# Half-steps in three 256-column matmuls a block, one block of output columns after the other

## The chip, the cores and the metric

The kernel runs on one core of one Trainium2 chip. The metric is the device time of one execution, in microseconds (us); shorter is better. A core has a matrix engine (PE; its weight loads are listed apart as PEld), a vector engine (DVE), a scalar engine (ACT), a general engine (POOL) and a queue that issues transfers (SP). They run side by side and wait for each other through semaphores. PE writes its sums into PSUM, eight banks of 512 float32 columns on each of 128 partitions; everything else lies in SBUF.

## What is computed

A decoder trunk of two layers over 256 tokens of width 1024. Each layer is a half-step, a mixer (latent attention in layer 0, forgetting attention in layer 1), a second half-step and a gated embedding. The part that the change is about, cut from the reference:

```python
def swiglu(x, w_in, w_out):                 # D_MODEL 1024, D_FF 2816
    gate, up = jnp.split(x @ w_in, 2, axis=-1)
    return (jax.nn.silu(gate) * up) @ w_out

for i in range(DEPTH):                      # DEPTH 2
    h = h + 0.5 * swiglu(rms_norm(h, g_ffn1[i]), ffn1_w_in[i], ffn1_w_out[i])
    h = h + mixer(rms_norm(h, g_mix[i]))    # latent (i = 0) or forgetting (i = 1)
    h = h + 0.5 * swiglu(rms_norm(h, g_ffn2[i]), ffn2_w_in[i], ffn2_w_out[i])
    h = h + sigmoid(rms_norm(h, g_ple[i]) @ ple_w_gate[i]) * (p[i] @ ple_w_proj[i])
```

All inputs are float32. There are four half-steps, and in each the products with `w_in` and `w_out`.

## The kernel before

**Three products for one.** Each float32 factor is split into a high part (rounded to fp32r) and a low part (the rest): a weight into `whi` and `wlo`, an activation into two planes `x[:, k, 0]` and `x[:, k, 1]`, 256 tokens each, next to each other in SBUF. A product is hi·hi + hi·lo + lo·hi, and low times low is dropped. The residual `h` is kept transposed, features on partitions and the 256 tokens in the columns, so a weight block of 128 rows by 128 output columns is the stationary operand (loaded by LDWEIGHTS), and the activation streams past it. What follows calls one weight block, at one k (row of blocks) and one b (block of output columns), simply a block.

**Weights.** `Weights` cuts all weights into units, mostly 1024 rows by 256 columns (8 k by 2 b, 16 blocks). `_load` brings a unit in on SP's queue, `_split` makes `whi` by ACT (L86) and `wlo` by DVE (L87) in pieces of 1024 columns. There are six buffers of each, three units' worth. `get()` hands out the next unit and first lets the unit two further on be split, so a split waits for the buffers of the unit just used.

**A half-step** is `ffn` (L423). Stage one runs over f = 0..10: a unit of gate columns and a unit of up columns, 8 k each, summed in PSUM. `part` (L420) calls `by_width` (L238): first all high blocks, k outside and the two b inside, each in one matmul of 512 columns that streams both activation planes into a bank of its own (hi·hi in the left half, hi·lo in the right, L255); then all low blocks in matmuls of 256 columns onto the right half (L248). `wide` (L417) gives a PSUM tile of two banks for that, one for the gate and one for the up unit; the pool `psa` has two such tiles. `summed` takes a result out: ACT copies the left halves (L431), DVE adds the right halves, and DVE and ACT go on from SBUF (`gate`, `product`). The products are split again into `hid`. Stage two runs over dp = 0..3, 256 output columns each, 22 k in units of 8, 8 and 6, in the same way from `hid`; its result is summed, scaled, added to `h`, and `after.chunk(dp)` prepares two rows of the next norm's input `xa`.

The kernel opens with f = 0 of the first half-step, in chunks of two k as `x` is turned (L1120 and after); its eviction follows once the root mean squares are known.

**Elsewhere** the kernel already uses `mm_w` (L231), three matmuls of 256 columns a block: hi·hi and hi·lo with the high block, loaded for each, and lo·hi. This is so in the latents `zmm` of the latent mixer (k outside, b inside), in the output projection `OutProj` of both mixers (k outside, four or eight column blocks inside) and in the gated embedding `ple` of layer 0 (b outside, k inside). `mm_x` (L262) has the operands swapped, with the activation stationary.

**Order.** Instructions are written in program order, and Tile adds the semaphores. `steady` and `order` keep marked instructions in the order written (all matmuls of a half-step among them); the rest may be moved by its planner. PSUM tiles are also drawn from `psb`, four banks.

Of the kernel before, what the change touches and what calls it, by code (L numbers as in the profile page):

```python
# [9 lines left out]
F32 = mybir.dt.float32  # L10
# [3 lines left out]
ALU = mybir.AluOpType  # L14
AX = mybir.AxisListType

P = 128
S = 256
D = 1024
KD = D // P  # L20
FF = 2816
KF = FF // P
# [129 lines left out]
def trunk(ctx: ExitStack, tc: tile.TileContext, a: dict, out: bass.AP):  # L152
    nc = tc.nc
# [10 lines left out]
    def pa():  # L164
        return psa.tile([P, 1024], F32, name="pa", tag="pa")

    def pb():
        return psb.tile([P, 512], F32, name="pb", tag="pb")
# [5 lines left out]
    w = Weights(nc, order, queue, raw, split, 2)  # L174
# [21 lines left out]
    for i in range(2):  # L196
# [22 lines left out]
        pg = a["ple_w_gate"][i]  # L219
# [9 lines left out]
    steady = Order(tc)  # L229

    def mm_w(ps, wt, cols, x, k, start, stop):  # L231

        hi, lo = wt[0][:, cols], wt[1][:, cols]
        steady(nc.tensor.matmul(ps, lhsT=hi, rhs=x[:, k, 0, :], start=start, stop=False, skip_group_check=True))  # L234
        steady(nc.tensor.matmul(ps, lhsT=hi, rhs=x[:, k, 1, :], start=False, stop=False, skip_group_check=True))  # L235
        return steady(nc.tensor.matmul(ps, lhsT=lo, rhs=x[:, k, 0, :], start=False, stop=stop, skip_group_check=True))  # L236

    def by_width(pss, wt, x, ks, first, last, at=0):  # L238


        out = None
        for low in range(2):
            for k in ks:
                for b, ps in enumerate(pss):
                    cols = slice(b * P, (b + 1) * P)
                    if low:
                        out = steady(
                            nc.tensor.matmul(  # L248
                                ps[:, 1, :], lhsT=wt(k)[1][:, cols], rhs=x[:, at + k, 0, :], start=False, stop=(k == last),
                                skip_group_check=True,  # L250
                            )
                        )
                    else:
                        steady(
                            nc.tensor.matmul(  # L255
                                ps, lhsT=wt(k)[0][:, cols], rhs=x[:, at + k], start=(k == first), stop=False, skip_group_check=True
                            )
                        )
        return out

    def mm_x(ps, wt, x, k, tt, start, stop):

        t = slice(tt * P, (tt + 1) * P)
# [5 lines left out]
    start = ExitStack()  # L269
# [26 lines left out]
    def small_loads():  # L296
# [22 lines left out]
        out=upper, in_=upper, compare_op=ALU.is_ge, fill=0.0, base=0, pattern=[[1, P]], channel_multiplier=-1  # L319
# [4 lines left out]
        out=mask[:, P:], in_=mask[:, P:], compare_op=ALU.is_ge, fill=NEG, base=0, pattern=[[-1, P]], channel_multiplier=1  # L324
# [23 lines left out]
    def tt_op(o, x, y, op):  # L348
        return nc.vector.tensor_tensor(o, x, y, op=op)  # L349
# [63 lines left out]
    def two(r):  # L413
        return r.unsqueeze(1).broadcast_to([P, 2, S])


    def wide():  # L417
        return pa().rearrange("p (b a t) -> p b a t", b=2, a=2)

    def part(ps, wt, x, ks):  # L420
        return by_width([ps[:, b] for b in range(2)], wt, x, ks, 0, KD - 1).ins

    def ffn(norm, after, fpool, beside={}, opened=None):  # L423

        steady.on = True
        x = norm.x
        hid = fpool.tile([P, KF, 2, S], F32R, name="hid", tag="hid", bufs=1)
        r = rh = None
        def summed(ps, name):
            o = fpool.tile([P, 2, S], F32, name=name, tag=name)  # L430
            nc.scalar.copy(o, ps[:, :, 0, :])  # L431
            tt_op(o, ps[:, :, 1, :], o, ALU.add)
            return o

        def gate(gt):
            tt_op(gt, gt, two(r), ALU.mult)
            nc.scalar.activation(gt, gt, AF.Silu)  # L437

        def product(f, gt, hf):
            tt_op(hf, gt, hf, ALU.mult)  # L440
            nc.scalar.copy(hid[:, 2 * f : 2 * f + 2, 0, :], hf)  # L441
            return tt_op(hid[:, 2 * f : 2 * f + 2, 1, :], hf, hid[:, 2 * f : 2 * f + 2, 0, :].bitcast(F32), ALU.subtract)

        for f in range(KF // 2):
            if f == 0:
                if opened:
                    pg, pu, pieces, roots, copies = opened
                    gt = summed(pg, "gt")
                    for _ in pieces:
                        pass  # L450
                    first = gt, summed(pu, "hf")
                    roots()
                    beside[0](None, None)
                    continue
                else:
                    pg, wg = wide(), w.get()
                    pu, wu = wide(), w.get()
                    part(pg, wg, x, range(6))
                    part(pu, wu, x, range(6))
                    part(pg, wg, x, range(6, KD))  # L460
                    order.on = True
                    r = norm.spread()
                    last = part(pu, wu, x, range(6, KD))
            else:
                pg = wide()
                if f == 1 and opened:
                    w.get(), w.get()
                part(pg, w.get(), x, range(KD))
                if f == 1 and opened:
                    r = roots()  # L470
                    gate(first[0])
                    product(0, *first)
                    copies()
            if f == 0 or f == 1 and opened:
                rh = stat.tile([P, S], F32, name="rh", tag="rh")
                nc.vector.tensor_scalar(rh, r, HALF, None, op0=ALU.mult)
            gt = summed(pg, "gt")
            gate(gt)
            if f:
                pu = wide()  # L480
                last = part(pu, w.get(), x, range(KD))
            hf = summed(pu, "hf")
            low = product(f, gt, hf)
            if f == 1:
                order.on = False
            if f in beside:
                beside[f](last, low.ins)
        for dp in range(4):
            ps = wide()
            for k0 in range(0, KF, 8):  # L490
                wt = w.get()
                by_width([ps[:, b] for b in range(2)], wt, hid, range(min(8, KF - k0)), -k0, KF - 1 - k0, k0)
            ot = summed(ps, "ot")
            tt_op(ot, ot, two(rh), ALU.mult)
            c = slice(2 * dp, 2 * dp + 2)
            tt_op(h[:, c, :], h[:, c, :], ot, ALU.add)
            after.chunk(dp)
        steady.on = False
# [71 lines left out]
    class OutProj:  # L570
# [9 lines left out]
        def first(self):  # L580

            for half in range(2):
                wt = w.get()
                for k in range(4):
                    for b in range(4):
                        self.mm(wt(k), k, half * 4 + b, b * P)
                        yield 3 * PASS
            wt = w.get()
            for k in range(2):
                for j in range(KD):  # L590
                    self.mm(wt(k), 4 + k, j, j * P)
                    yield 3 * PASS

        def rest(self):
            wt = w.get()
            for dp in range(4):
                for k in range(2):
                    for j in (2 * dp, 2 * dp + 1):
                        self.mm(wt(k), 6 + k, j, j * P)
                c = slice(2 * dp, 2 * dp + 2)  # L600
                b = 2 * (dp % 2)
                tt_op(h[:, c, :], h[:, c, :], self.ps[dp // 2][:, b : b + 2, :], ALU.add)
                self.after.chunk(dp)
# [139 lines left out]
    def mla(norm, after, pool):  # L743
        x = norm.x
# [4 lines left out]

        def zmm(c, wt, ks):  # L750

            for k in ks:
                for b in range(2 if c < 3 else 1):
                    mm_w(
                        zps[c // 2][:, 2 * (c % 2) + b, :], wt(k), slice(b * P, (b + 1) * P), x, k,
                        start=(k == 0 and b == 0), stop=(k == KD - 1),
                    )
# [21 lines left out]
        for ks in (range(6), range(6, KD)):  # L779
            zmm(2, wa, ks)  # L780
            zmm(3, wb, ks)
# [29 lines left out]
        skv, rh = rs[:, :2], rs[:, 2:]  # L811
# [17 lines left out]
        got, ready = {}, set()  # L829
# [7 lines left out]
        o = act.tile([P, KD, 2, S], F32R, name="xa", tag="xa")  # L837
# [299 lines left out]


    norm = Norm(0, 0)
    pg, pu = wide(), wide()  # L1140
    turned = []

    def turn(dp):
# [52 lines left out]
    def copies():  # L1196
        for dp in range(1, 4):
            order((nc.scalar.copy if dp > 1 else nc.vector.tensor_copy)(h[:, 2 * dp : 2 * dp + 2, :], turned[dp]))
# [84 lines left out]
```

## Time and profile before

| | |
|---|---|
| Median of 3 runs | 1048.88 us (1048.74 to 1050.88) |
| The profiled execution | 1048.94 us, of which its span is 1047.2 us |
| PE busy | 1033.1 us, 99% of the span, 6380 matmuls |
| DVE, ACT, POOL busy | 777.6, 599.6, 77.3 us |
| Granted TensorE clock over the span | 0.998 |

Three views serve below. The list of waits says how long an engine stood still and for whom. A timeline lists instructions in order of their start; matmuls overlap in it (a matmul's duration runs to the end of its last column), so what a stream of matmuls costs is read from one start to the next, not from the durations. The table by stretch gives the busy time of an engine and the granted clock between two times, and counts each instruction that reaches into the stretch.

### The profile page before, as it was taken

What the parts mean: (1) busy time and instruction counts of PE and PEld (TensorE: products, weight loads), DVE (VectorE), ACT (ScalarE), POOL (GpSimd) and SP (SyncE); (2) the same over time, 40 slices, a digit from 0 to 9 for tenths busy, and PEclk for the clock granted to TensorE, in tenths of its full rate; (3) what the DMA queues carried; (4) which work ended last, traced back from release to release, by engine and by line L of the source; (5) the groups of instructions that cost most, each with busy time, mean ns of one, the idle gap of its engine ahead of it and who ended that gap; (6) DMA issues with size and microseconds to landing.
All of it is one profiled execution on the core that took longest, in us unless ns stands there. A gap on an engine that the chain in (4) does not pass through costs nothing.

```text
span 1047.2 us, 16326 instructions
## 1 busy us (share of the span) xinstructions
PE 1033.1 (99%) x6380; PEld 918.7 (88%) x6380; DVE 777.6 (74%) x1369; ACT 599.6 (57%) x903; POOL 77.3 (7%) x99
## 2 busy tenths in 40 slices
PE   8999999999999999999999999999999999999998
PEld 7888888987898888889888888899998888888886
DVE  5988756689979777666987776658788797776664
ACT  6666544558766555455656554535655666554452
POOL 0000000243120000001100000001000200000010
PEclk9999999999999999999999999999999999999999
DMA  7775555534336655556547555554643357555551
GB/s 243 245 236 184 176 179 172 181 97 163 114 100 200 221 184 188 189 180 205 171 147 243 178 188 179 181 154 144 229 141 102 105 188 237 182 174 189 181 161 41
DMA packets 171105, 182.60 MB, mean 174 GB/s; under 512 B 6094, under 2 KB 164372, under 8 KB 171028
## 3 DMA queue, kind: packets, MB, share of 16 engines
q1 hardware_dynamic: 170452, 181.03, 53.8%
q8 instruction: 50, 0.82, 0.3%
q10 hardware_dynamic: 576, 0.53, 0.1%
q14 instruction: 27, 0.22, 0.1%
HBM read 180.50 MB, written 1.05 MB: 173 GB/s over the span
## 4 chain that ended last, share of the span: by engine, by line
PE 95%; DVE 3%; DMA 1%; issue 0%; ACT 0%; POOL 0%; ACTq 0%; DVEq 0%
PE pa L255 46%; PE pa L248 24%; PE pa L264 3%; PE pa L266 3%; PE pa L265 3%; PE pa L234 2%; PE pa L236 2%; PE pa L235 2%; DVE wlo L87 1%; PE pb L611 1%; PE pb L518 1%; PE pb L558 1%; PE pb L546 1%; PE pb L517 1%; DMA xn<-in_x_dram 1%; PE pb L266 1%
## 5 line engine op out<-in xcount | busy, mean ns | idle before, releaser
L87 DVE TENSOR_TENSOR wlo<-raw,whi 128x1024 fp32r<-128x1024 f32 (+2 forms) x351 | 417.8, 1220 | 171.4 <-PE pa L248 73.6
L86 ACT CAST whi<-raw 128x1024 fp32r<-128x1024 f32 (+2 forms) x351 | 351.0, 1016 | 246.8 <-PE pa L255 180.4
L255 PE MATMUL pa<-xa,whi 128*128 128x512 f32 x1408 | 342.6, 394 | 2.3 <-DVE xa L376 2.3
L255 PEld LDWEIGHTS pa<-xa,whi 128*128 128x128 f32 x1408 | 257.8, 188 | 54.3 <-DVE xa L376 3.5
L248 PEld LDWEIGHTS pa<-xa,wlo 128*128 128x128 f32 x1408 | 177.8, 188 | 8.6
L248 PE MATMUL pa<-xa,wlo 128*128 128x256 f32 x1408 | 179.4, 278 | 0.0
L255 PE MATMUL pa<-hid,whi 128*128 128x512 f32 x704 | 168.7, 391 | 0.0
L255 PEld LDWEIGHTS pa<-hid,whi 128*128 128x128 f32 x704 | 129.1, 188 | 24.8
L384 POOL TENSOR_TENSOR sq<-sq 128x512 f32<-128x512 f32 x21 | 37.9, 1805 | 826.7 <-ACT sq L382 799.9
L248 PEld LDWEIGHTS pa<-hid,wlo 128*128 128x128 f32 x704 | 90.8, 191 | 3.7
L248 PE MATMUL pa<-hid,wlo 128*128 128x256 f32 x704 | 91.9, 283 | 0.0
L264 PE MATMUL pa<-whi,xa 128*128 128x256 f32 (+3 forms) x192 | 59.1, 308 | 0.0
L266 PE MATMUL pa<-whi,xa 128*128 128x256 f32 (+3 forms) x192 | 57.7, 301 | 0.0
L265 PE MATMUL pa<-wlo,xa 128*128 128x256 f32 (+3 forms) x192 | 57.4, 299 | 0.0
L234 PE MATMUL pa<-xa,whi 128*128 128x256 f32 x184 | 54.3, 295 | 0.0
L349 DVE TENSOR_TENSOR hid<-hf,hid 128x512 fp32r<-128x512 f32 x44 | 30.5, 692 | 29.0 <-ACT hid L441 29.0
L236 PE MATMUL pa<-xa,wlo 128*128 128x256 f32 x184 | 51.9, 283 | 0.0
L235 PE MATMUL pa<-xa,whi 128*128 128x256 f32 x184 | 51.8, 282 | 0.0
L431 ACT COPY gt<-pa 128x512 f32<-128x512 f32 x44 | 25.8, 587 | 36.8 <-PE pa L248 36.8
L431 ACT COPY hf<-pa 128x512 f32<-128x512 f32 x44 | 25.8, 585 | 28.9 <-PE pa L248 28.9
L437 ACT ACTIVATE gt<-gt 128x512 f32<-128x512 f32 x44 | 27.6, 627 | 19.3 <-DVE gt L349 19.2
L264 PEld LDWEIGHTS pa<-whi,xa 128*128 128x128 f32 x192 | 36.1, 188 | 1.3 <-issue 0.5
(281 smaller groups left out, 1214.2 us busy)
## 6 DMA issues: line engine op xcount, KB each, us to landing
raw<-in_ffn_w_in_dram SPq DMA_DIRECT2D x86, 1024.0 KB, 5.1
raw<-in_ffn_w_out_dram SPq DMA_DIRECT2D x32, 1024.0 KB, 5.1
raw<-in_ffn_w_out_dram SPq DMA_DIRECT2D x16, 768.0 KB, 4.6
raw<-in_ple_w_gate_dram SPq DMA_DIRECT2D x8, 1024.0 KB, 5.2
raw<-in_fox_w_in_dram SPq DMA_DIRECT2D x8, 1024.0 KB, 5.7
raw<-in_mla_w_o_dram SPq DMA_DIRECT2D x4, 1024.0 KB, 5.5
raw<-in_fox_w_o_dram SPq DMA_DIRECT2D x4, 1024.0 KB
raw<-in_mla_w_in_dram SPq DMA_DIRECT2D x3, 1024.0 KB, 6.7
```

Source lines behind the costliest of these rows:

```text
L86: self.order(self.nc.scalar.copy(h, whole))
L87: self.order(self.nc.vector.tensor_tensor(low, whole, h.bitcast(F32), op=ALU.subtract))
L234: steady(nc.tensor.matmul(ps, lhsT=hi, rhs=x[:, k, 0, :], start=start, stop=False, skip_group_check=True))
L235: steady(nc.tensor.matmul(ps, lhsT=hi, rhs=x[:, k, 1, :], start=False, stop=False, skip_group_check=True))
L236: return steady(nc.tensor.matmul(ps, lhsT=lo, rhs=x[:, k, 0, :], start=False, stop=stop, skip_group_check=True))
L248: nc.tensor.matmul(ps[:, 1, :], lhsT=wt(k)[1][:, cols], rhs=x[:, at + k, 0, :], start=False, stop=(k == last), skip_group_check=True,)
L255: nc.tensor.matmul(ps, lhsT=wt(k)[0][:, cols], rhs=x[:, at + k], start=(k == first), stop=False, skip_group_check=True)
L264: steady(nc.tensor.matmul(ps, lhsT=x[:, k, 0, t], rhs=wt[0], start=start, stop=False, skip_group_check=True))
L265: steady(nc.tensor.matmul(ps, lhsT=x[:, k, 0, t], rhs=wt[1], start=False, stop=False, skip_group_check=True))
L266: steady(nc.tensor.matmul(ps, lhsT=x[:, k, 1, t], rhs=wt[0], start=False, stop=stop, skip_group_check=True))
L384: nc.gpsimd.tensor_tensor(sq, sq, self.acc, op=ALU.add)
L431: nc.scalar.copy(o, ps[:, :, 0, :])
```

## The change

`by_width`, `wide` and `summed` go. A half-step's block is now the three 256-column matmuls of `mm_w`, and `part` runs b outside and k inside: all rows of the first block of 128 output columns, then all of the second. Both b share one bank. Gate and up share one `psa` tile (`step_banks`: a bank each), the second stage takes its tile from `psb`. DVE multiplies straight from PSUM (`gate`, `product` and the scaling of stage two), without ACT's copy and DVE's add. The first evictions of the opening come after the roots. The latents (`zmm`) and `OutProj` also put b (j) outside and k inside. Cut to its core:

```diff
-    def by_width(pss, wt, x, ks, first, last, at=0):
...
-    def wide():
-        return pa().rearrange("p (b a t) -> p b a t", b=2, a=2)
-    def part(ps, wt, x, ks):
-        return by_width([ps[:, b] for b in range(2)], wt, x, ks, 0, KD - 1).ins
+    def step_banks():
+        ps = pa().rearrange("p (u b t) -> p u b t", u=2, b=2)
+        return ps[:, 0], ps[:, 1]
+    def part(ps, wt, x, ks, first=0, last=KD - 1, at=0):
+        for b in range(2):
+            for k in ks:
+                got = mm_w(
+                    ps[:, b, :], wt(k), slice(b * P, (b + 1) * P), x, at + k, start=(k == first and b == 0), stop=(k == last)
+                )
+        return got.ins
...
-        def summed(ps, name):
-            o = fpool.tile([P, 2, S], F32, name=name, tag=name)
-            nc.scalar.copy(o, ps[:, :, 0, :])
-            tt_op(o, ps[:, :, 1, :], o, ALU.add)
-            return o
-        def gate(gt):
-            tt_op(gt, gt, two(r), ALU.mult)
+        def gate(gt, ps):
+            tt_op(gt, ps, two(r), ALU.mult)
             nc.scalar.activation(gt, gt, AF.Silu)
-        def product(f, gt, hf):
-            tt_op(hf, gt, hf, ALU.mult)
+        def product(f, gt, ps, hf):
+            tt_op(hf, gt, ps, ALU.mult)
...
-                pg = wide()
+                first = pg, pu
+                pg, pu = step_banks()
...
-            gt = summed(pg, "gt")
-            gate(gt)
+            gt, hf = pair_of()
+            gate(gt, pg)
             if f:
-                pu = wide()
                 last = part(pu, w.get(), x, range(KD))
-            hf = summed(pu, "hf")
-            low = product(f, gt, hf)
+            low = product(f, gt, pu, hf)
...
-            ps = wide()
+            ps = pb().rearrange("p (b t) -> p b t", b=2)
             for k0 in range(0, KF, 8):
-                wt = w.get()
-                by_width([ps[:, b] for b in range(2)], wt, hid, range(min(8, KF - k0)), -k0, KF - 1 - k0, k0)
-            ot = summed(ps, "ot")
-            tt_op(ot, ot, two(rh), ALU.mult)
+                part(ps, w.get(), hid, range(min(8, KF - k0)), -k0, KF - 1 - k0, k0)
+            ot = fpool.tile([P, 2, S], F32, name="ot", tag="ot")
+            tt_op(ot, ps, two(rh), ALU.mult)
...
-                for k in range(4):
-                    for b in range(4):
+                for b in range(4):
+                    for k in range(4):
                         self.mm(wt(k), k, half * 4 + b, b * P)
...
-            for k in ks:
-                for b in range(2 if c < 3 else 1):
+            for b in range(2 if c < 3 else 1):
+                for k in ks:
```

## Rows read from the trace of the kernel before

**Rows 1.** The page's busy times, and its chain that ended last, by engine.

```profile
PE   1033.1 (99%) x6380; PEld 918.7 (88%) x6380; DVE 777.6 (74%) x1369; ACT 599.6 (57%) x903; POOL 77.3 (7%) x99
...
PE 95%; DVE 3%; DMA 1%; issue 0%; ACT 0%; POOL 0%; ACTq 0%; DVEq 0%
```

**Rows 2.** Longest wait of PE in the span: total us, times, longest us.

```profile
PE pa L255 <- DVE xa L376: 2.3, 1, 2.3
```

**Rows 3.** Table by stretch, PE: stretch, its us, busy (count), clock, DMA.

```profile
33.34:133.04 99.70, 99.70 (x580) 1.00 0.66 212
133.04:194.29 61.25, 61.25 (x354) 1.00 0.58 179
328.77:428.07 99.30, 99.30 (x579) 1.00 0.65 208
```

**Rows 4.** PE's stage-one high matmuls as a group: count, busy, mean ns, idle.

```profile
L255 PE MATMUL pa<-xa,whi 128*128 128x512 f32 x1408 | 342.6, 394 | 2.3 <-DVE xa L376 2.3
```

**Rows 5.** Timeline of PE in stage one: start us, us to the end.

```profile
33.34 3.82 PE L255 MATMUL pa<-xa,whi 128*128 128x512 f32 x16
37.00 2.04 PE L248 MATMUL pa<-xa,wlo 128*128 128x256 f32 x16
38.88 3.84 PE L255 MATMUL pa<-xa,whi 128*128 128x512 f32 x16
42.56 1.98 PE L248 MATMUL pa<-xa,wlo 128*128 128x256 f32 x16
44.37 3.82 PE L255 MATMUL pa<-xa,whi 128*128 128x512 f32 x16
```

**Rows 6.** Timeline of PE in stage two.

```profile
138.60 3.82 PE L255 MATMUL pa<-hid,whi 128*128 128x512 f32 x16
142.26 2.08 PE L248 MATMUL pa<-hid,wlo 128*128 128x256 f32 x16
144.17 2.91 PE L255 MATMUL pa<-hid,whi 128*128 128x512 f32 x12
```

**Rows 7.** Table by stretch, PE, unbroken 256-column streams: zmm, ple (two), fox.

```profile
194.41:208.42 14.01, 14.01 (x121) 1.00 0.50 148
489.44:494.97 5.53, 5.53 (x49) 1.00 0.62 203
498.62:517.54 18.92, 18.92 (x169) 1.00 0.52 168
711.51:722.46 10.95, 10.95 (x95) 1.00 0.53 169
```

**Rows 8.** Timeline of PE's weight loads inside ple's stream.

```profile
498.96 0.19 PEld L236 LDWEIGHTS pb<-xa,wlo 128*128 128x128 f32 x1
499.07 0.19 PEld L234 LDWEIGHTS pb<-xa,whi 128*128 128x128 f32 x1
```

**Rows 9.** Groups of ACT and DVE by line: what takes a result out.

```profile
L431 ACT COPY gt<-pa 128x512 f32<-128x512 f32 x44 | 25.8, 587 | 36.8 <-PE pa L248 36.8
L349 DVE TENSOR_TENSOR gt<-pa,gt 128x512 f32<-128x512 f32 x44 | 30.1, 684 | 2.7 <-ACT gt L431 2.7
```

**Rows 10.** Waits of PE from 703 to 712 us.

```profile
PE pb L406 <- POOL ss L388: 1.1, 1, 1.1
```

**Rows 11.** Timeline of PE where the second layer begins.

```profile
517.54 2.00 PE L255 MATMUL pa<-xa,whi 128*128 128x512 f32 x8
521.81 1.19 PE L255 MATMUL pa<-xa,whi 128*128 128x512 f32 x4 [2.27 <-DVE xa L376]
```

**Rows 12.** Table by stretch: PE in the last output projection of layer 0.

```profile
302.98:305.33 2.35, 2.35 (x22) 1.00 0.97 324
```

**Rows 13.** Timeline of DVE in that stretch.

```profile
304.12 0.69 DVE L349 TENSOR_TENSOR h<-h,pa 128x512 f32<-128x512 f32 x1 [0.25 <-PE pa L236]
```

**Rows 14.** Groups of DVE and ACT by line: the splits of the weights.

```profile
L87 DVE TENSOR_TENSOR wlo<-raw,whi 128x1024 fp32r<-128x1024 f32 (+2 forms) x351 | 417.8, 1220 | 171.4 <-PE pa L248 73.6 <-ACT whi L86 59.3 <-issue 38.1
L86 ACT CAST whi<-raw 128x1024 fp32r<-128x1024 f32 (+2 forms) x351 | 351.0, 1016 | 246.8 <-PE pa L255 180.4 <-issue 27.8 <-PE pa L266 11.2
```

More of the change, by code (lines that the diff above doesn't have):

```diff
@@ L236, in mm_w @@
         return steady(nc.tensor.matmul(ps, lhsT=lo, rhs=x[:, k, 0, :], start=False, stop=stop, skip_group_check=True))
-    def by_width(pss, wt, x, ks, first, last, at=0):
-        out = None
-        for low in range(2):
-            for k in ks:
[L244 to L259, printed above, removed]
     def mm_x(ps, wt, x, k, tt, start, stop):
@@ L428, in ffn, with pair_of @@
         r = rh = None
-        def summed(ps, name):
-            o = fpool.tile([P, 2, S], F32, name=name, tag=name)
-            nc.scalar.copy(o, ps[:, :, 0, :])
-            tt_op(o, ps[:, :, 1, :], o, ALU.add)
-            return o
-        def gate(gt):
-            tt_op(gt, gt, two(r), ALU.mult)
+        def gate(gt, ps):
+            tt_op(gt, ps, two(r), ALU.mult)
             nc.scalar.activation(gt, gt, AF.Silu)
-        def product(f, gt, hf):
-            tt_op(hf, gt, hf, ALU.mult)
+        def pair_of():
+            return [fpool.tile([P, 2, S], F32, name=n, tag=n) for n in ("gt", "hf")]
+        def product(f, gt, ps, hf):
+            tt_op(hf, gt, ps, ALU.mult)
             nc.scalar.copy(hid[:, 2 * f : 2 * f + 2, 0, :], hf)
@@ L447, in ffn @@
                     pg, pu, pieces, roots, copies = opened
-                    gt = summed(pg, "gt")
                     for _ in pieces:
                         pass
-                    first = gt, summed(pu, "hf")
                     roots()
@@ L455, in ffn @@
                 else:
-                    pg, wg = wide(), w.get()
-                    pu, wu = wide(), w.get()
+                    pg, pu = step_banks()
+                    wg, wu = w.get(), w.get()
                     part(pg, wg, x, range(6))
@@ L464, in ffn @@
             else:
-                pg = wide()
+                first = pg, pu
+                pg, pu = step_banks()
                 if f == 1 and opened:
@@ L470, in ffn @@
                     r = roots()
-                    gate(first[0])
-                    product(0, *first)
+                    gt, hf = pair_of()
+                    gate(gt, first[0])
+                    product(0, gt, first[1], hf)
                     copies()
@@ L476, in ffn @@
                 nc.vector.tensor_scalar(rh, r, HALF, None, op0=ALU.mult)
-            gt = summed(pg, "gt")
-            gate(gt)
+            gt, hf = pair_of()
+            gate(gt, pg)
             if f:
-                pu = wide()
                 last = part(pu, w.get(), x, range(KD))
-            hf = summed(pu, "hf")
-            low = product(f, gt, hf)
+            low = product(f, gt, pu, hf)
             if f == 1:
@@ L588, in first @@
             wt = w.get()
-            for k in range(2):
-                for j in range(KD):
+            for j in range(KD):
+                for k in range(2):
                     self.mm(wt(k), 4 + k, j, j * P)
@@ L596, in rest @@
             for dp in range(4):
-                for k in range(2):
-                    for j in (2 * dp, 2 * dp + 1):
+                for j in (2 * dp, 2 * dp + 1):
+                    for k in range(2):
                         self.mm(wt(k), 6 + k, j, j * P)
@@ L750, in zmm @@
         def zmm(c, wt, ks):
-            for k in ks:
-                for b in range(2 if c < 3 else 1):
+            for b in range(2 if c < 3 else 1):
+                for k in ks:
                     mm_w(
@@ L1139, in trunk @@
     norm = Norm(0, 0)
-    pg, pu = wide(), wide()
+    pg, pu = step_banks()
     turned = []
```

## The prediction

> **What bounds the kernel now.** I read the page first: PE is busy for 99% of the span and makes 95% of the chain that ended last [rows 1]; DVE and ACT have a quarter and two fifths of the span to spare. Then the waits of PE: the longest in the whole span is 2.3 us [rows 2]. Then the table by stretch: from 33.34 to 133.04 us PE is busy for all of 99.70 us, at a granted clock of 1.00 (the 2.4 GHz level), and for all of 61.25 us after that; the other half-steps look the same [rows 3]. So a half-step is as long as its matmuls take to stream, and nothing that DVE or ACT is spared inside one shortens it. What the change is worth hangs on the pace of matmuls, from one start to the next.
>
> A unit of stage one is 16 high matmuls of 512 columns and 16 low ones of 256. From starts [rows 5]: high 3.66 us (37.00 - 33.34) or 3.68 (42.56 - 38.88), low 1.88 (38.88 - 37.00) or 1.81 (44.37 - 42.56). So 512 columns take 229 ns, and 256 columns take 117.5 or 113.1 ns: units alternate between the two. The stretch from 328.77 to 428.07 holds 18 units, 5.517 us each [rows 3], or 344.8 ns a block. In stage two [rows 6]: high 3.66 us, low 1.91 (144.17 - 142.26), so 229 and 119.4 ns; a whole stage two is 61.25 us for 176 blocks, 348.0 ns each.
>
> **The change, part by part.**
>
> *The matmuls.* A block streamed 512 + 256 columns and will stream 3 x 256: the same columns, with one more instruction and one more weight load. What counts is whether two 256-column matmuls cost more than one of 512. The trace has unbroken streams of 256 columns elsewhere [rows 7] (two of each count began before its stretch): 14.01 us for 119 in `zmm`, 117.7 ns; 5.53 us for 47 in `ple`'s first product, 117.7; 18.92 us for 167 in `ple`'s gates, 113.3; 10.95 for 93 of `mm_x`, 117.7. They fall into the two paces that the low units also have. `ple` has b outside and k inside, as the change will have, and runs at either pace, so the loop order doesn't choose between them. A stream keeps its pace through many units; which it takes follows from how it was entered.
>
> The third weight load itself is hidden: in `ple`'s stream loads of 0.19 us start 0.11 us apart [rows 8], at the pace of the matmuls, one under the matmul before it. Were they not, each would cost up to 0.19 us; the streams above have that in them, so they are the bound that I use.
>
> Stage one then: 22 units in a half-step, 88 in all (the 1408 high matmuls of [rows 4] over 16), with f = 0 and 1 taken at the same pace. A unit will be 48 matmuls: at 113.3 ns 5.438 us, 0.078 less than 5.517, so -6.9 us over 88; at 117.7 ns 5.650, 0.133 more, so +11.7 us. No row says which pace a stream of 960 matmuls takes that starts behind the norm's reduction. The stream behind that same reduction in `ple` ran at 113.3; the others in the rows were slower. I take half and half: +2.4 us.
>
> Stage two: 528 matmuls a half-step. Low matmuls on `hid` never show the two paces but 119.4 ns, one pattern for all twelve low groups of a half-step [rows 6]. At that, 63.04 us against 61.25: +1.8 each, +7.2 us for four. At 113.3 it would be 59.82, -5.7 us for four; at 117.7, +3.6. I take 119.4, the only rows with this operand.
>
> *Evictions.* ACT's copy (587 ns) and DVE's add (684 ns) go [rows 9], 104 of each over the four half-steps (22 and 4 in each): 61 us of ACT, 71 us of DVE. The scaling by DVE that stays now reads PSUM; the add that goes read PSUM too, for 684 ns, so I put no extra on it. All of that is hidden behind PE. It shows only where PE waits for the end of a half-step: once, 1.1 us for the sum of squares early in the forgetting mixer [rows 10]. That chain gets 1.27 us shorter (0.587 + 0.684), so this wait goes: -1.1 us, and PE itself is late next there. The other half-steps have no such wait to give.
>
> *PSUM.* Gate and up get a tile for both, so two f are in flight instead of one; stage two moves to the other pool. DVE will read the gate's bank while PE writes the up bank of the same tile. `OutProj` does just that now: DVE reads one half of a tile at 304.12 us [rows 13] while 20 matmuls go on in 2.35 us, 117.5 ns each [rows 12]. No wait, cost 0.
>
> *Order.* With k inside, the first column block asks for all its rows of `xa` at once. At the start of the second layer PE does 8 matmuls and then stands 2.27 us for the next rows [rows 11]. Before that stop fit 8 high matmuls, 1.83 us; then 12 of 256 columns, 1.4 us, so PE gets there 0.45 us sooner and has that much more to do after: +0.5 us. At the other two such starts I allow 0 to 0.5 us each, and take 0.3. In `zmm` and `OutProj` the number and width of matmuls stay. What `zmm` asks for sooner (k = 4, 5) was done a column block of stage two earlier (61.25 / 4 = 15 us), and `OutProj`'s units come up only when the head pairs that they need are mixed, so no wait is added. A flip of pace there would be 168 or 192 matmuls by 4.4 ns, 0.8 us either way, and I take 0. No transfer and no instruction of SP moves past another.
>
> *Splits.* A piece of `whi` is now held until 36 or 48 of 48 matmuls are done, not until 8 or 16 of 32, so ACT, which waits for these buffers already [rows 14], begins a unit's casts up to 2.3 us later. Two casts (1.02 us each) and two subtractions (1.22) are 4.5 us, used two units (11 us) after the buffers come free. The unit in between hides it; without that cover PE would wait up to 2.3 us a unit.
>
> Sum: 2.4 + 7.2 - 1.1 + 0.5 + 0.6 = +9.6 us. The profiled execution is 1048.94 us (span 1047.2 and 1.7 around it), 0.06 over the median, so it stands for the median: **1058.5 us**. About 0.2% (2.1 us) is what a measurement of this kernel can tell from no change.
>
> **The rivals.**
>
> *All slow.* Every stage one at 117.7 ns: 11.7 + 7.2 + 0 = +18.9, **1067.8 us**. For it: three of the four streams in [rows 7]. Against it: half of the low units, and `ple` behind the reduction.
>
> *Fast input, slow `hid`.* -6.9 + 7.2 + 0 = +0.3, **1049.2 us**, no change.
>
> *All fast (the other side).* Once at 113.3 ns the stream keeps that pace through `hid` as well: -6.9 - 5.7 + 0 = -12.6, **1036.3 us**. It decides from where a stream on `hid` runs below 348.0 / 3 = 116.0 ns. For it: 113.3 ns held over 167 matmuls. Against it: the low groups on `hid`, which are all at 119.4.
>
> *A fixed small price for an instruction.* If the two paces are only scatter around one, every 256 columns cost their mean, 115.5 ns, on either operand: two of them are 2.0 ns over 229, and 2112 blocks add 4.2 us, with the other parts at 0 **1053.1 us**. For it: the mean of the low units in [rows 5]. Against it: each stream holds its pace, and `hid` has its own. The Trainium skill has such a rule, "TensorE: Matmul & The Clock Gate", section "Back-to-back issue gap": the columns at 2.4 GHz and some 2.5 ns for each matmul. By it the sum would be 2112 x 2.5 ns = +5.3 us, 1054.2 us, and a 256-column matmul 109.2 ns, an estimate from that page; no stream here runs at that.
>
> *A new wait*, for a late split or for a bank of the shared tile: at least DVE's 0.68 us for each of 40 f, over +27 us, **1086 us**; [rows 12] speak against it.
>
> **How the numbers follow.** Forecast 0.45 (1055 to 1063), all slow 0.20, fast input with slow `hid` 0.10, all fast 0.15, fixed price 0.06, new wait 0.04. Faster: all fast, and 0.02 of the third case, 0.17. Same: the rest of that case, 0.08. Slower: 0.75. The range reaches from near all fast, left out, to all slow: 1040 to 1068 leaves out 0.14 below and 0.04 and a little of the slow case above.
>
> **What would show it.** In the trace after, starts of matmuls in stage one 113 or 118 ns apart, 18 units of stage one in 97.9 to 101.7 us against 99.3, each stage two in 62 to 63.4 against 61.25. PE still without waits in half-steps, the 1.1 us wait gone, the 2.27 us one some 0.5 longer. ACT 61 and DVE 71 us less busy, with no effect. It would be wrong if `hid` streams below 116 ns, or if PE waits for weights or for DVE inside an f.

## The result, and where the time went

| | Kernel before | Changed kernel |
|---|---|---|
| Median (same chip) | 1049.39 us | 1145.82 us (1141.29 to 1150.86) |
| Profiled execution, its span | 1048.94, 1047.2 us | 1141.29, 1139.5 us |
| Ratio to before | | 1.0914 (95%: 1.0897 to 1.0930) |

Slower by 9%, far above the range of the prediction (1040 to 1068 us). In one of the four runs of the variant with the late read, below, the granted clock was 0.600 and the time 1589 us; that run and its trace are left out.

First the page of the changed kernel: busy times, and the chain that ended last, by engine.

```profile
PE 1059.1 (93%) x8492; PEld 1025.1 (90%) x8492; DVE 700.8 (62%) x1265; ACT 550.4 (48%) x799; POOL 70.6 (6%) x99
...
PE 80%; DVE 11%; ACT 5%; issue 1%; DMA 1%; ACTq 0%; SPq 0%; DVEq 0%
```

Against [rows 1] PE is busy for 26 us more but makes only 80% of the chain: it now stands still for 80 us of the span. DVE and ACT became less busy by 77 and 49 us (71 and 61 forecast), and yet DVE has come into the chain. The waits of PE (total us, times, longest us) say where:

```profile
PE pa L234 <- DVE gt L326: 61.7, 39, 2.4
...
PE pb L497 <- ACT qt L595: 2.2, 3, 0.8
PE pa L234 <- ACT xa L351: 2.0, 3, 1.2
PE pa L234 <- DVE rt L635: 1.8, 1, 1.8
...
PE pa L235 <- DVE xa L353: 0.6, 1, 0.6
```

The first line is nearly all of it (L326 is the helper through which DVE's products and sums go; here it reads the gate's sum). The fourth line is one more stop of the same kind (the profile puts it down to a table that DVE worked on at the time), so there are 40 stops: one for each f = 1 to 10 in four half-steps. 36 of them are 1.60 to 1.81 us long, the first of the kernel 2.37, and the other three at an f = 1 0.87. From the last start before a stop to the first one after it, the 40 stops come to 74.7 us, where 40 steps of 118 ns would be 4.7 us; the next matmul then came 195 ns later in place of 118, 3.1 us more in all. So the stops cost 70.0 + 3.1 = 73.1 us of the 92.35 between the two profiled executions.

One of them, a timeline of all engines (PE's even stream and its weight loads left out):

```profile
93.01 1.05 ACT L86 CAST whi<-raw 128x1024 fp32r<-128x1024 f32 x1 [1.90 <-PE pa L235]
...
94.09 1.23 DVE L87 TENSOR_TENSOR wlo<-raw,whi 128x1024 fp32r<-128x1024 f32 x1 [1.89 <-ACT whi L86]
94.18 0.28 PE L236 MATMUL pa<-xa,wlo 128*128 128x256 f32 x1
...
95.23 0.68 DVE L326 TENSOR_TENSOR gt<-pa,r 128x512 f32<-128x512 f32 x1
...
96.06 0.36 PE L234 MATMUL pa<-xa,whi 128*128 128x256 f32 x1 [1.60 <-DVE gt L326]
```

The gate unit's last matmul starts at 94.18 and ends at 94.46. The up unit's first one, ready to go, starts at 96.06, 0.15 us after DVE has read the gate's sum. It writes the other bank of the tile; it waits for the read all the same. DVE comes to that read late: ahead of it in its queue stands a split of weights (94.09 to 95.32), which waited for ACT's cast, which waited for PE to let go of a piece of `whi`. That is the late split that the prediction described (a piece is held until 36 of 48 matmuls are done), and so a stop is two parts: the rest of a 1.23 us subtraction and 0.68 us of multiply.

The rest of the forecast can be read from two rows of the table by stretch (us, PE busy, count, clock, DMA): a stage two, and 972 matmuls of a stage one.

```profile
154.04:217.40 63.36, 63.36 (x531) 1.00 0.55 171
...
341.22:472.66 131.44, 115.99 (x974) 1.00 0.53 168
```

A stage two streams without a gap for 63.36 us (61.25 in [rows 3]), 120.0 ns a matmul. The stage one of 131.44 us holds 15.4 us of standing.

### The profile page after: what moved, and what is told of

It is laid out like the page before. It is cut to its first block, busy times and chain, and to the rows that moved or that the text cites. A ratio compares the mean times of both kernels' runs of the same rounds, so it can differ in the third digit from the quotient of the medians.

```text
span 1139.5 us, 20348 instructions
## 1 busy us (share of the span) xinstructions
PE 1059.1 (93%) x8492; PEld 1025.1 (90%) x8492; DVE 700.8 (62%) x1265; ACT 550.4 (48%) x799; POOL 70.6 (6%) x99
## 4 chain that ended last, share of the span: by engine, by line
PE 80%; DVE 11%; ACT 5%; issue 1%; DMA 1%; ACTq 0%; SPq 0%; DVEq 0%
PE pa L234 15%; PE pa L235 14%; PE pa L236 14%; PE pb L235 8%; PE pb L234 8%; PE pb L236 8%; DVE wlo L87 6%; ACT whi L86 4%; PE pa L241 3%; PE pa L243 3%; PE pa L242 3%; DVE gt L326 2%; DMA raw<-in_ffn_w_in_dram 1%; PE pb L591 1%; PE pb L538 1%
## 5 line engine op out<-in xcount | busy, mean ns | idle before, releaser
L234 PE MATMUL pa<-xa,whi 128*128 128x256 f32 x1592 | 452.1, 284 | 67.2 <-DVE gt L326 61.7
L235 PE MATMUL pa<-xa,whi 128*128 128x256 f32 x1592 | 444.8, 279 | 1.0 <-DVE xa L353 0.6
L236 PE MATMUL pa<-xa,wlo 128*128 128x256 f32 x1592 | 444.4, 279 | 0.0
L234 PEld LDWEIGHTS pa<-xa,whi 128*128 128x128 f32 x1592 | 299.3, 188 | 77.3 <-ACT whi L86 64.8
L235 PEld LDWEIGHTS pa<-xa,whi 128*128 128x128 f32 x1592 | 299.2, 188 | 2.5 <-DVE xa L353 1.5
L236 PEld LDWEIGHTS pa<-xa,wlo 128*128 128x128 f32 x1592 | 299.6, 188 | 0.7 <-issue 0.7
L234 PE MATMUL pb<-hid,whi 128*128 128x256 f32 x704 | 199.2, 283 | 0.0
L236 PE MATMUL pb<-hid,wlo 128*128 128x256 f32 x704 | 199.2, 283 | 0.0
L235 PE MATMUL pb<-hid,whi 128*128 128x256 f32 x704 | 199.2, 283 | 0.0
L236 PEld LDWEIGHTS pb<-hid,wlo 128*128 128x128 f32 x704 | 135.2, 192 | 0.0
L234 PEld LDWEIGHTS pb<-hid,whi 128*128 128x128 f32 x704 | 135.2, 192 | 0.0
L235 PEld LDWEIGHTS pb<-hid,whi 128*128 128x128 f32 x704 | 135.1, 192 | 0.0
L351 ACT ACTIVATE xa<-h,gvec 128x256 fp32r<-128x256 f32 x56 | 25.4, 500 | 31.3 <-DVE h L326 31.3
L424 ACT CAST hid<-hf 128x512 fp32r<-128x512 f32 x44 | 27.4, 622 | 20.2 <-DVE hf L326 20.1
```

Source lines behind the costliest of these rows:

```text
L351: order(nc.scalar.activation(self.x[:, c, 0, :], h[:, c, :], AF.Copy, scale=g))
```

## The experiments

The theory from here on, **A**: the up unit waits because gate and up share one tile, and reads and writes are ordered by tile. The rivals, in which the tile has no part: **B**, it is the late split of the weights that holds PE; **C**, DVE's straight read of one bank holds up PE's writes to the next. Ratios are to the kernel before on the same chip.

**Own tiles (e1).** From the changed kernel:

```diff
...
-                pg, pu = step_banks()
+                pg = own_tile()
...
             if f:
+                pu = own_tile()
                 last = part(pu, w.get(), x, range(KD))
```

> The changed kernel, but for f >= 1 (and for f = 0 of the three later half-steps) the gate and the up unit have a PSUM tile each, as in the kernel before; all matmuls, loop orders and evictions are as changed. Theory A (the up unit's first matmul waits for DVE's read of the gate because both lie in one tile): PE's 40 stops of about 1.84 us (1.88 and 0.20 for two starts where 0.12 each would do) go, 74 us, so about 1068 to 1072 us, near the forecast's slow end. Theory B (PE waits because the splits of the weights come late): the stops stay, over 1120 us. Theory C (DVE's read of one bank holds up PE's writes to the next): the stops stay too, as DVE reads at the same moment.

1097.41 us, ratio 1.0454 (1.0434 to 1.0473). 48 of the 96 us come back, fewer than A said. The stops inside the half-steps are gone, but four longer ones are there, at f = 1. The waits of PE, and the table by stretch around one:

```profile
PE pa L234 <- DVE gt L326: 16.7, 4, 4.6
```

```profile
328.51:333.37 4.86, 0.28 (x3) 0.78 0.66 211
333.37:341.00 7.63, 7.63 (x47) 0.69 0.17 48
341.00:360.00 19.00, 19.00 (x164) 1.00 0.62 203
```

There are two such tiles in all, so the gate of f = 1 needs the tile of the gate of f = 0. DVE reads that one only when it has worked out the norm's roots: PE stands for 4.58 us. In the kernel before ACT's copy emptied that tile without the roots. After the stop the granted clock is lower (0.69): 20 of the next matmuls start some 213 ns apart, which is 256 columns at the 1.2 GHz level. No stop of 1.6 us in the changed kernel was followed by that. Three such stops cost 4.9 us each, and the slow matmuls behind them 5.4 us more in all; the first f = 1 of the kernel cost 3.2 and 1.4 us. That makes 24 of the 25 us by which e1 lies above what A said.

**Late read (e2).** The changed kernel, tiles as they are, but the read of the gate written behind the up unit:

```diff
-            gt, hf = pair_of()
-            gate(gt, pg)
             if f:
                 last = part(pu, w.get(), x, range(KD))
+            gt, hf = pair_of()
+            gate(gt, pg)
```

> The changed kernel with its shared tile, but the gate is read (multiplied, silu) only after the up unit's matmuls in program order. Theory A: the up unit no longer has a read of its tile ahead of it, so the stops go here as well, about 1068 to 1072 us, as without the shared tile. Theory B: no change, 1140 us or more, as no split is moved ahead. Theory C: between the two; the read now falls beside the next gate unit.

1073.98 us (median of its other three runs), ratio 1.0227 (1.0210 to 1.0244). 72 us come back, a little less than A said, with the tile still shared and the reads still straight from PSUM. Only the place of the read was changed: it now stands behind the up unit's matmuls, and behind the split that their `w.get()` queues. That split can come sooner by the one read, 0.68 us, which is too little for B where a stop costs 1.83. That the stops are gone is read from the time alone here; e5 shows it in a trace.

**Single banks (e5).** Every gate and every up sum in a one-bank tile of its own, four of them, so that two f stay in flight (in the first half-step from f = 2 on, since `x` still holds those banks):

```diff
...
-                pg, pu = step_banks()
+                pg, pu = step_banks() if opened and f == 1 else (bank(), bank())
...
-            ps = pb().rearrange("p (b t) -> p b t", b=2)
+            ps = pa()[:, : 2 * S].rearrange("p (b t) -> p b t", b=2)
```

> The changed kernel, but from the second half-step's opening on (and from f = 2 in the first) the gate and the up sums of a unit lie in two one-bank tiles of their own; stage two takes its bank from the other pool instead. The order of all instructions as written, the reads straight from PSUM and the banks in flight (two f) stay as in the changed kernel. Theory (the up unit's first matmul waits for the read of the gate sum because both are one tile): the stops of 1.6 us behind the gate units go, and since two f stay in flight nothing replaces them: 1049.7 + 6.6 (stage two alone) + 5.75 (order alone) + 9 to 12 (stage one at 117.7 ns) = 1071 to 1074 us. Rival (the stop comes from reading PSUM straight, or from the late split of the weights): stops stay, 1130 to 1146 us.

1076.79 us, ratio 1.0259 (1.0244 to 1.0274), 69 us less than the changed kernel. Waits of PE, and a stage one of 972 matmuls, the one that took 131.44 us above:

```profile
PE pa L234 <- DVE gt L326: 2.9, 1, 2.9
```

```profile
325.23:439.90 114.67, 114.67 (x974) 1.00 0.57 188
```

The one stop left is the first half-step's f = 1, which still shares its tile (3.2 us more between two starts, and 1.4 us for 15 matmuls at the 1.2 GHz level behind it); the expected 1071 to 1074 us had left it out. Everything else of theory A holds. The order as written, the splits and the straight reads are those of the changed kernel, so B and C fall: reading one bank while PE writes another costs nothing here (972 matmuls in 114.67 us without a gap), if they are two tiles. The Trainium skill, "PSUM — Partial Sum Buffer", section "PSUM bank collisions raise a hardware error", asks for guards by bank and quadrant; the shared tile was guarded more widely than that, and e5 shows what the narrower guard is worth, 69 us.

That leaves some 27 us without any shared tile. The next runs take it apart, each from the kernel before.

**Stage two alone (e3).** `part` with three matmuls in place of `by_width`, no sum:

> The kernel before with the second stage alone changed (three 256-column matmuls a block from hid, b outside, tile from psb, no sum). The forecast's term: 528 matmuls at 119.4 ns in place of 61.25 us, +7.2 us for four half-steps, less 1.1 us for the wait in the forgetting mixer: about 1055.5 us. Rival (hid streams at 113.3 ns once no 512-column matmul comes between): -5.7 - 1.1 us, about 1042.5.

1056.32 us, ratio 1.0064 (1.0048 to 1.0081): +6.6 against +6.1 forecast.

**Order alone (e4),** in the latents and the output projection:

> The kernel before with the loop order of the latents and of the output projection alone changed (b or j outside, k inside). The forecast: 0, with 0.8 us either way for a flip of pace, 1048.5 to 1050. Rival: k inside asks for late rows sooner, and PE waits at the start of a latent or projection: +1 to +3 us.

1055.49 us, ratio 1.0057 (1.0042 to 1.0072): +5.75, where I had put 0 for these two and the rival 1 to 3. Waits of PE that the kernel before doesn't have, or has less of in total, from the list of e4:

```profile
PE pa L255 <- DVE xa L376: 3.2, 3, 1.8
...
PE pb L517 <- ACT qt L615: 2.0, 3, 0.8
...
PE pa L235 <- DVE xa L376: 0.8, 1, 0.8
PE pa L234 <- DVE h L349: 0.8, 2, 0.4
PE pa L234 <- DVE ka L349: 0.7, 1, 0.7
```

**Latents' order alone (e7).**

```diff
-            for k in ks:
-                for b in range(2 if c < 3 else 1):
+            for b in range(2 if c < 3 else 1):
+                for k in ks:
```

> The kernel before with only the latents' loop order changed (b outside, k inside). Theory: of the 5.75 us that the order cost in latents and output projection together, the latents have the one wait that the trace shows there, 0.8 us for a row of the norm's input: 1050.2 to 1051.0 us; the rest, near 5 us, is the output projection asking for head pairs that are not yet mixed. Rival (a changed order costs by its pace or loads wherever it is): half or more of it here, 1052.5 us or above.

1051.10 us, ratio 1.0015 (1.0006 to 1.0025): +0.6 to +2.6 us. That is at the upper edge of the theory's 1050.2 to 1051.0 us and below the rival's 1052.5. Its trace has the one wait of the latents: the first column block asks for the last two rows of `xa`, which DVE has ready at 201.79 us.

```profile
201.84 0.38 PE L235 MATMUL pa<-xa,whi 128*128 128x256 f32 x1 [0.80 <-DVE xa L376]
```

The other 4 us or so are left for the output projection, by difference; no run changes its order alone, and what follows is read from the waits of e4. With k inside, its first column block runs through all head pairs at once, and those of the later ones are not mixed yet. Its matmuls are what the planner fills PE with while head pairs are turned and weighed; when fewer of them can go, PE waits for `qt` and `ka` (the rows above), and both following half-steps begin 0.7 us late on `xa`. The two waits for `h` are the shared tile again: an `OutProj` tile holds the columns of two dp, and the matmuls into its second half wait until DVE has read the first half into `h`.

**Stage one alone (e6),** with e5's tiles; stage two, latents and output projection as before:

```diff
...
-                pg = wide()
+                first = pg, pu
+                pg, pu = step_banks() if opened and f == 1 else (bank(), bank())
...
-            gt = summed(pg, "gt")
-            gate(gt)
+            gt, hf = pair_of()
+            gate(gt, pg)
```

> The kernel before with only stage one in three 256-column matmuls a block, b outside, gate and up in one-bank tiles of their own, read without a sum; stage two, the latents and the output projection as before. Theory: the parts add up, so this is what is left of the late-read variant: 1074.3 - 6.6 - 5.75 = 1061.9 us, 1060 to 1063, with stage one's streams mostly 117.7 ns from start to start. Rival (stage one as the forecast had it, half of the units at 113.3 ns): 1052 us, and the late-read variant's remainder lies in parts acting on each other.

1064.18 us, ratio 1.0138 (1.0123 to 1.0153): +14.5, against +12.2 expected. The stop at the first f = 1 is in it (3.2 us, and 1.5 for 16 matmuls at the 1.2 GHz level; the expectation had overlooked it), so the pace of stage one is worth about 10 us. Table by stretch, 576 and 972 matmuls:

```profile
72.53:140.47 67.94, 67.94 (x577) 1.00 0.55 181
323.33:438.00 114.67, 114.67 (x974) 1.00 0.58 189
```

Both are 118.0 ns a matmul. So the parts add up: 1049.7 + 6.6 + 5.75 + 14.5 = 1076.6 us against 1076.79 for e5, and with 73.1 us of stops less the 4.6 of e5's own, 1145.1 against 1145.82. That last agreement is closer than the numbers can bear: the changed kernel's four runs lie 9.6 us apart.

**What sets the 120.0 ns on `hid`.** No unbroken stream on `xa` ran at that. In the layout of the kernel both buffers of `xa` begin at a multiple of 512 bytes within a partition, `hid` 192 bytes past one. Three runs move it, each from e3 (e8 with 320 empty bytes ahead of `hid`, e10 with 512, e11 with 64):

```diff
+        fpool.tile([P, 80], F32, name="pad", tag="pad", bufs=1)
         hid = fpool.tile([P, KF, 2, S], F32R, name="hid", tag="hid", bufs=1)
```

> The variant with only stage two in three matmuls (1056.3 us, 120.0 ns from start to start on hid), with 320 bytes left empty ahead of hid in each partition, so that hid begins at a multiple of 512 bytes as both buffers of xa do, and not 192 bytes past one. Theory P (the pace of a stream follows from where its operand lies): 113.3 to 117.7 ns, 2112 matmuls by 2.3 to 6.7 ns less, 1042 to 1051.5 us. Rival (the pace has another cause): 120.0 ns and 1056 to 1057 us again.

> Only stage two in three matmuls, with 512 empty bytes ahead of hid: hid and all behind it move by more than in the aligned variant, but hid begins 192 bytes past a multiple of 512 again. Theory P (it is the position within 512 bytes): 120.0 ns on hid and 1056 to 1057 us, as without the empty bytes. Rival (any move of hid or of what lies behind it breaks the pattern): 113.3 to 117.8 ns and 1046 to 1052 us.

> Only stage two in three matmuls, with 64 empty bytes ahead of hid, which then begins 256 bytes past a multiple of 512. It tells how coarse the position counts. If a multiple of 256 bytes is enough: 113.3 to 117.8 ns on hid, 1046 to 1052 us. If it must be a multiple of 512, or if only a larger move matters: 120.0 ns, 1056 to 1057 us.

A stage two of 528 matmuls in each, from the tables by stretch: e8 (the first two), e10, e11 (the first and the third).

```profile
133.98:193.82 59.84, 59.84 (x530) 1.00 0.57 182
426.98:489.17 62.19, 62.19 (x531) 1.00 0.54 178
```

```profile
134.11:197.46 63.35, 63.35 (x530) 1.00 0.55 173
```

```profile
134.30:194.14 59.84, 59.84 (x530) 1.00 0.58 181
639.21:701.39 62.18, 62.18 (x530) 1.00 0.53 170
```

| `hid` begins | ns a matmul, four stage twos | Median, ratio |
|---|---|---|
| 192 past 512 (e3) | 120.0 in all | 1056.32, 1.0064 (1.0048 to 1.0081) |
| 192 past 512, moved by 512 (e10) | 120.0 in all | 1057.69, 1.0074 (1.0060 to 1.0088) |
| at 512 (e8) | 113.3, 117.8, 117.8, 117.8 | 1049.47, 1.0003 (0.9985 to 1.0021) |
| 256 past 512 (e11) | 113.3, 113.3, 117.8, 117.8 | 1048.65, 0.9990 (0.9974 to 1.0007) |

The move alone does nothing, the position does: from 192 to 0 or 256 the 120.0 ns are gone, and `hid` has the two paces of `xa`.

But 192 by itself is not enough. The buffers of the weights, `whi` and `wlo`, begin 192 bytes past a multiple of 512 as well, in all these kernels. In `mm_x` it is the weights that stream, 256 columns of them past an `xa` that begins at 0, and no such stream ran at 120.0: one took 117.7 ns in the kernel before ([rows 7], the last), and this one in e3 took 113.4 (94 matmuls from start to start, table by stretch):

```profile
717.41:728.07 10.66, 10.66 (x95) 1.00 0.53 174
```

What the streams at 120.0 ns have to themselves is that both operands, `hid` and the weight block loaded for it, begin 192 past. Whether it is that pair or something else about `hid` at 192, no run here tests; moving the weights' buffers would.

Which of the two paces of `xa` a stage two takes isn't settled by the address, since one kernel has both. It may differ between executions too: e8's ten runs lie 7.4 us apart (1045.88 to 1053.23), those of the kernel before beside them 2.6; only the profiled execution shows paces, so that stays a guess.

**The same empty bytes in the kernel before (e9).**

> The kernel before with nothing changed but the 320 empty bytes ahead of hid, which put its start at a multiple of 512 bytes. Theory P (the address sets the pace): the low matmuls on hid, 704 of them at 119.4 ns, come to 113.3 or 117.8 as in the variant with stage two alone, 1.1 to 4.3 us less, and the 512-column matmuls stay at 229 ns: 1045.4 to 1048.6 us. Rival (the empty bytes help only through the three matmuls in a row): 1049.7 us, no change.

1048.09 us against 1050.06, ratio 0.9978 (0.9969 to 0.9987): 0.2% faster. Low matmuls on `hid` in it, the timeline of PE (1.91 us for a group of 16 in [rows 6]):

```profile
137.90 2.05 PE L248 MATMUL pa<-hid,wlo 128*128 128x256 f32 x16
139.78 3.84 PE L255 MATMUL pa<-hid,whi 128*128 128x512 f32 x16
143.46 1.98 PE L248 MATMUL pa<-hid,wlo 128*128 128x256 f32 x16
145.27 1.07 PE L255 MATMUL pa<-hid,whi 128*128 128x512 f32 x4
```

1.88 and 1.81 us a group, 117.5 and 113.1 ns a matmul: the two figures that the low units on `xa` have in [rows 5].

**With the short chain where it is waited for (e12).** e9, and the change kept for 256 output columns, dp = 3 of the second layer's first half-step:

```diff
+            if short and dp == 3:
+                ps = pb().rearrange("p (b t) -> p b t", b=2)
+                for k0 in range(0, KF, 8):
+                    part256(ps, w.get(), hid, range(min(8, KF - k0)), -k0, KF - 1 - k0, k0)
+                ot = fpool.tile([P, 2, S], F32, name="ot", tag="ot")
+                tt_op(ot, ps, two(rh), ALU.mult)
```

> The kernel before with the 320 empty bytes ahead of hid, and with one thing of the change kept where its shorter chain is waited for: the last 256 output columns (dp = 3) of the second layer's first half-step in three 256-column matmuls a block, evicted without a copy and a sum. Theory: PE's wait of 1.1 us for the sum of squares in the forgetting mixer goes, 44 blocks cost between 0 and +0.4 us: 1047.0 to 1047.5 us against 1048.1 with the empty bytes alone. Rival (something else is late there at once): the wait comes back under another name, 1048.1 us or more.

1046.85 us against 1049.83, ratio 0.9970 (0.9958 to 0.9982): 3 us faster than the kernel before, and the best of all. The wait for the sum of squares [rows 10] is not in its list any more. Whether it beats e9 too is open: the two intervals overlap.

## Why the prediction was wrong, step by step

**The step that failed** is "PSUM": "No wait, cost 0". It cost 73.1 us. The reason was a row misread. [rows 12, 13] show DVE reading `pa` while 20 matmuls go on writing `pa`, and I took both for one tile. The rows leave buffer numbers out, and `OutProj` has two such tiles (`self.ps[dp // 2]`). In the program as built, its planner works on them in turn: DVE's four reads take the first tile, the second, the first, the second, and the 12 matmuls that go on from 303.92 us, beside the read at 304.12, write the tile that is not being read. The first matmul into a tile's other half does wait for the read of the first half there; that read was merely done in time. In a half-step `steady` fixes PE's order, gate then up. Nothing in the trace of before showed a read and a write of the same tile side by side, and then the cost had to be bounded by what a wait would cost.

**The rival "a new wait"** had the count, 40 f, and the mechanism, "a bank of the shared tile", at a price of at least 0.68 us each. The price was 1.83, because the split ahead of the read belongs to it. I had given it a chance of 0.04.

**"Splits"** said that the unit in between hides the later casts. For PE's weights that is true: without the shared tile PE never waits for them (e5). But I looked at who waits for the split, not at what stands behind it in DVE's queue.

**"Stage two"** was right: +7.2 forecast for four, 4 x (63.36 - 61.25) = +8.4 in the trace, +6.6 by e3 with the 1.1 us wait gone. "Low matmuls on `hid`" kept their own pace, as I took it; that it hangs on the place of `hid` I did not see. *All fast* was no idle rival: e11's two stage twos at 59.84 us ran at its pace, though none did where `hid` lies in the changed kernel. No stream came to the 109.2 ns by which the fixed price was worked out from the Trainium skill ("TensorE: Matmul & The Clock Gate", section "Back-to-back issue gap"): 113.3 is the fastest here. The section gives that formula for a matmul by itself and not for a stream.

**"Stage one"** was mis-sized within its bounds: +2.4 taken, about +10 measured (e6), near the end of +11.7. In the changed kernel about a fifth of the matmuls on `xa` ran at 113.3, in e6 nearly none.

**"Order"** was mis-sized: 0 for latents and output projection, with 0.8 either way; +5.75 measured. The argument "units come up only when the head pairs that they need are mixed" holds for a unit and not for the first column block in it; and of the rows that `zmm` asks for sooner I had looked at k = 4 and 5, not at the last two. The starts of the half-steps, at +1.1 us, were put too high: the waits for `xa` there come to 2.6 us in the changed kernel, against 2.3 before.

**"Evictions"** was right. The 1.1 us wait in the forgetting mixer is gone in the changed kernel and in e3. But ACT's copy had a second use that I did not name: it frees the gate's tile before the roots are there (e1).

Without the shared tile the forecast would have been too low still, 1058.5 against 1074 to 1077, from the order and stage one, and in e5 from the stop at the first f = 1.

## What to carry to other kernels

Two sums that are read at different times belong in two tiles, even when they lie in two banks (or the read behind both, as in e2): with a shared tile the writer of the second waits for the reader of the first, and for all that stands ahead of that reader in its queue. An eviction that needs nothing from elsewhere (a plain copy) frees its tile earlier than a fused one, so before a copy is saved, look at what the fused read waits for. A row that seems to show two engines on one tile shows only one name; find out which buffer it is before a cost of 0 is built on it.

## What the hardware did that I had not expected

- A 256-column fp32r stream has three paces here: 113.3, 117.8 and 120.0 ns. 120.0 came in every stage two of such matmuls whose `hid` began 192 bytes past a multiple of 512 bytes, where the weight blocks begin too; it came in none whose `hid` began at 0 or 256, and in no stream of weights at 192 past an `xa` at 0. Where it came it cost 2.2 to 6.7 ns a matmul. The Trainium skill, "SBUF — State Buffer", section "Operand start alignment", asks that an operand begin at a multiple of its element size, 4 bytes for float32. It says that this is about what is allowed and not about speed; 192 is allowed by it, as 0 and 256 are.
- Between 113.3 and 117.8 no run here chooses, but a stream keeps the one that it has until something breaks it. In the changed kernel two f, each from one stop's end to the next, hold 96 matmuls each, the first at 117.7 ns and the second at 113.3 throughout (busy time less 0.19 us for the first step and 0.28 for the last matmul, over the 94 steps between):

```profile
43.43:56.58 13.15, 11.54 (x96) 1.00 0.51 164
56.58:69.37 12.79, 11.12 (x96) 1.00 0.51 162
```

- After PE had stood for 4.58 us, the granted clock was 0.69 over the next 7.6 us (e1), with 20 matmuls at the 1.2 GHz level. The 36 stops of 1.6 to 1.8 us in the changed kernel left its mean clock at 0.998.
